# A transformer layer with a planned instruction order: GpSimd's queue in the plan, fewer gathers of softmax statistics, rows of the first norm moved to the gate products, earlier value sums, and the square root's table asked for ahead

## The chip, the cores and the metric

The kernel runs on one core of one Trainium2 chip. The metric is the device time of one execution in microseconds (us). The engines are TensorE (PE: matmuls and transposes, with PEld for its weight loads), VectorE (DVE), ScalarE (ACT), GpSimd (POOL) and SyncE (SP). SP does nothing here but issue DMA transfers, in a fixed order; POOL issues DMAs too, and hardly anything else. Every engine works through its own instructions strictly in order: where one waits, all behind it wait.

## The reference, cut to what matters

One layer over 1024 positions of width 1024 in fp32: a feed-forward part and norm 1, a mixer of attention and Fourier branch and norm 2, a second feed-forward part and norm 3.

```python
def swiglu(x, w_gate, w_up, w_down):
    return (jax.nn.silu(x @ w_gate) * (x @ w_up)) @ w_down          # inner width 2752

def hybrid_mixer(x, ...):
    h = x @ w_in + b_in                     # q, k, v (12 heads of 128), fourier channels, gates
    gates = jax.nn.sigmoid(...)
    for g, (window, dilation) in enumerate(((128, 1), (512, 4), (2048, 16))):
        o, l = dilated_window_attention(q_g, k_g, v_g, rel_bias_g, window, dilation)   # 4 heads
    w_mix = jax.nn.softmax(jnp.stack(lses, axis=0), axis=0)   # weights of the three groups
    attn = jnp.sum(w_mix[..., None] * jnp.stack(outs, axis=0), axis=0)
    four = jnp.real(jnp.fft.fft2(uf, axes=(1, 3), norm='ortho'))
    merged = g_attn * (attn @ w_proj_attn) + g_four * (four @ w_proj_fourier)
    return merged @ w_out

h = layer_norm(ALPHA * h + 0.5 * swiglu(h, ffn1...), ln1_g, ln1_b)
h = layer_norm(ALPHA * h + hybrid_mixer(h, ...), ln2_g, ln2_b)
h = layer_norm(ALPHA * h + 0.5 * swiglu(h, ffn2...), ln3_g, ln3_b)
```

## The kernel before, in words

**Products.** Each large product is cut into 2 x 2 blocks and done in seven block products, as in Strassen's scheme. They need sums of weight blocks and sums of products. An fp32 operand is split into a high and a low part (`ga` becomes `ga12h` on ACT and `ga12l` on DVE), and PE multiplies high by high, low by high and high by low. `Aa`, `Ab`, `Da`, `Db`, `Aq`, `Dq` are PSUM banks of such products; `t2a`, `t3a`, `sga` and the like are copies and sums that ACT and DVE make of them. `tpZ` and `pt` are transposes on PE. In the names, the first feed-forward part carries `a` at the end, the second `b`, the queries and keys `q`.

**Stages.** First feed-forward part (0 to about 580 us of the profile), with gate and up products in chunks, each chunk with weights `ga` and `ua` that SP loads; norm 1; values (`v`); queries, keys and attention together, head by head (about 820 to 1145); the gate products (about 1145 to 1280) with the Fourier branch's work after them; the output projection `wo` with norm 2 (about 1400 to 1470); the second feed-forward part and norm 3.

**Sums in DRAM.** Some sums of weight blocks are made by transfers: SP copies a block to a scratch tensor and POOL adds a second block by an accumulating DMA. `tdat` and `tdbt` are the sums for the down products, `vtt` those for the values (`t1`, `t3`, `t2`, `t4`, where `t2` starts from `t1` and `t4` from `t2`). A copy that starts from an earlier sum waits on SP's queue until that sum has landed.

**Attention.** Per head: scores (`sc`) on PE, bias and maximum on DVE (`p`, `stat`), exponentials on ACT (`p<-p,stat`), transposes of `p` on PE (`pt`), copies by ACT (`pT`), products with the values (`pv`). The maxima and sums go to DRAM (`stat`), and come back in another layout by gathers (`comb_t`); DVE and ACT make from them the weights of the three groups (`comb`), which are stored, broadcast over the partitions by POOL's DMA (`cb`) and multiplied into the stored outputs on DVE (`pw<-pw,cb`).

**Norm rows.** Norm 1 leaves rows without gain and bias in DRAM. Eight steps of `norm_rows` load such a tile `n`, multiply by the gain and add the bias on DVE, and spill it as `y_spill` from POOL's queue for the residual sum before norm 2.

**What sets the order.** The class `Flow` runs at build time. The code registers jobs of PE, tasks of DVE (`V`) and ACT (`S`), loads (`Q`) and floating PE work (`F`), with a cost in us, what they depend on, and a need: the job they must be ready for. `Flow` walks through the jobs with a clock for each of DVE and ACT and one for the transfers, picks the next task that is ready, and calls its function, which emits its instructions. The costs only order the instructions; nothing of them is executed. Buffers are counted in the same walk: 46 pages of 128 x 1024, 11 halves, 8 PSUM banks. A DMA that POOL issues was an ACT task of cost 0:

```python
n = S(0.0, lambda: nc.gpsimd.dma_start(dst, st["y"]), [n])
```

Of the kernel before, what the change touches and what calls it, by code (L numbers as in the profile page):

```python
# [72 lines left out]
class Flow:  # L73
# [3 lines left out]
    def __init__(self):  # L77
        self.jobs, self.tasks, self.loads, self.floats = [], [], [], []
        self.open = {"V": [], "S": []}
        self.clock = {"V": 0.0, "S": 0.0}  # L80
        self.pe = self.dma = self.now = 0.0
        self.pool = {"b": [0.0] * 8, "p": [0.0] * NPG, "h": [0.0] * NS2}
# [15 lines left out]
    def S(self, *a, **kw):  # L98
        return self.task("S", *a, **kw)

# [65 lines left out]
    def issue(self):  # L166
        for n in list(self.loads):
# [10 lines left out]
            t = max(self.pe, n.time(), self.take(n))  # L178
            n.fn()
            self.dma = max(self.dma, t) + n.cost / self.RATE  # L180
            self.finish(n, self.dma + self.LAND)

    def advance(self, until):
        while True:
            e = min(("V", "S"), key=lambda k: self.clock[k])
# [17 lines left out]
            if best is None or best[1] > c + 0.05:  # L203
                o = self.clock["S" if e == "V" else "V"]
# [5 lines left out]
            self.take(n)  # L210
            n.fn()
            self.clock[e] = r + n.cost
# [26 lines left out]
    def run(self):  # L239
# [9 lines left out]
        for i in range(4000):  # L249
            if not (self.floats or self.loads or self.open["V"] or self.open["S"]):  # L250
                break
# [33 lines left out]
def kernel(  # L285
# [10 lines left out]
    V, S, Q, F, job = fl.V, fl.S, fl.Q, fl.F, fl.job  # L296
# [14 lines left out]
    nc.vector.memset(eps, LN_EPS)  # L311

# [294 lines left out]
    def ffn(tag, X, w_gu, w_tail, w_dn, load_rest, norm, rest_deps=None, sums_at=None, by_tile=False):  # L607
# [7 lines left out]
        def spill(name, j, t):  # L615
            nc.gpsimd.dma_start(hs[name, j], t)  # L616
# [152 lines left out]
        for si, (to, x0, x1) in enumerate(sums):  # L769
            for i in range(3):  # L770
# [3 lines left out]
                def add(to=to, x1=x1, i=i):  # L774
                    nc.gpsimd.dma_start(td[to, i], dn(x1, i), accum_op=OP.add, max_dma_last_dim=4096)
# [28 lines left out]
        def step(p, j, set_, first):  # L804
# [10 lines left out]
            return run  # L815

# [140 lines left out]

    def norm_head(acc, sums, deps, name, which):
# [17 lines left out]
    def norm_tile(acc, sums, deps, name, which):  # L976
# [10 lines left out]
        return S(1.08, scaled, [n], gives=1), lambda: st["y"]  # L987

    def norm_rows(which, m, src, deps, dst, need):
# [15 lines left out]
        n = S(0.0, lambda: nc.gpsimd.dma_start(dst, st["y"]), [n])  # L1005
# [55 lines left out]
    def norm1(m, acc, sums, deps):  # L1061
        n, y = norm_tile(acc, sums, deps, f"y1_{m}", 1)
        unit[1, m] = S(0.0, lambda: nc.gpsimd.dma_start(n_spill[m], y()), [n])
# [18 lines left out]
    def mixer_consts():  # L1082
        st = {}

        def loads():
            st["raw"] = half("b_raw")[:56, :P]
            nc.gpsimd.dma_start(st["raw"], b_in.rearrange("(j p) -> j p", p=P))
            st["rb"], st["oh"] = kb.small([NUM_BUCKETS, NH], "rb"), half("oh")[:NUM_BUCKETS, :3 * NOFF]
            nc.gpsimd.dma_start(st["rb"], rel_bias)
            nc.gpsimd.dma_start(st["oh"], c_onehot.rearrange("b g o -> b (g o)"))  # L1090
            nc.gpsimd.dma_start(chan, c_chan)
            nc.gpsimd.dma_start(ln_cols, c_ln)
# [9 lines left out]
        def lines(g):  # L1102
# [3 lines left out]
            nc.gpsimd.dma_start(lines_d[:, g, :], line)  # L1106

        def shears(h):
            src = lines_d[h, h // SLOTS, :]
            nc.gpsimd.dma_start(shear_d[h], bass.AP(tensor=src.tensor, offset=src.offset, ap=[[0, P], [1, LINE]]))  # L1110
        q = S(0.0, loads, [J[("a", 6), 1]], slack=20.0, halves=2)
# [5 lines left out]
        return [S(0.0, lambda h=h: shears(h), [(n, 6.0 + 3.0 * h)]) for h in range(NH)]  # L1117

    def reversed_rows():
        idx = kb.small([P, 2], "rev_idx", mybir.dt.int32)  # L1120
        st, n = {}, S(0.0, lambda: nc.gpsimd.dma_start(idx, c_rev), [J[("a", 8), 1]], slack=20.0)
        for t in range(2):
            def gather(t=t):
                st[t] = page(f"rev{t}")
                nc.gpsimd.indirect_dma_start(out=st[t], out_offset=None, in_=w_pf,
                                             in_offset=bass.IndirectOffsetOnAxis(ap=idx[:, t:t + 1], axis=0))

            def store(t=t):
                nc.gpsimd.dma_start(w_rev[t * P:(t + 1) * P, :], st[t])
            n = S(0.0, gather, [(n, 16.0)], slack=20.0, pages=1)  # L1130
            n = S(0.0, store, [(n, 16.0)], slack=20.0)
# [40 lines left out]
    for i, (to, x0, x1) in enumerate((("t1", "b11", "b12"), ("t3", "b12", "b22"), ("t2", "t1", "b22"),  # L1172
# [4 lines left out]
        def add(to=to, x1=x1):  # L1177
            nc.gpsimd.dma_start(vt[to], vblk[x1], accum_op=OP.add, max_dma_last_dim=4096)
        n = Q(J[("a", 7 + i), 1], 1.0, copy, [vtn[x0]] if x0 in vtn else [], lead=0.0)
        vtn[to] = Q(J[("a", 8 + i), 5], 1.0, add, [n], lead=0.0)  # L1180

    def value_row(key, g, need):
        def run():
            vb[key] = half(f"vb{key}")
            nc.gpsimd.dma_start(vb[key], bcast_rows(b_in[COL_V + g * 512:COL_V + (g + 1) * 512], 512))
# [9 lines left out]
    def store_values(t, m, g):  # L1195
        nc.gpsimd.dma_start(v_d[m * P:(m + 1) * P, g * 512:(g + 1) * 512], t)
# [176 lines left out]
    def channel_parts(gi, get, deps, gives):  # L1373
# [18 lines left out]
        def parts():  # L1392
# [13 lines left out]
            nc.gpsimd.dma_start(uf_d[gi], uf)  # L1406
# [31 lines left out]
    def load_bias(g, h):  # L1438
# [3 lines left out]
        def shear(dst, base, rows, w):  # L1442
            nc.gpsimd.dma_start(dst, bass.AP(tensor=src.tensor, offset=src.offset + base,
# [42 lines left out]
    def attention(idx, g, h, qk, qk_nodes):  # L1486
# [17 lines left out]
        def one(si, step):  # L1504
# [105 lines left out]
        pv_n[g, h] = S(0.0, lambda: nc.gpsimd.dma_start(pv_d[g, h], env["pv"]), done_values)  # L1610
# [15 lines left out]
    for c in range(8):  # L1626
        gs = {}
        nodes = pair_out(PC["s", c], [COL_G + c * P, COL_G + D + c * P], gs, plain_view, AF.Sigmoid)
        for w in range(2):
            gate_n[w, c] = S(0.0, lambda c=c, w=w, gs=gs: nc.gpsimd.dma_start(gate_d[w, c], gs[w]), nodes[w])  # L1630
            fl.later(gate_n[w, c], 5.0, gives=1)

# [20 lines left out]
    def keep_parts(name, load, deps, fold_=None):  # L1653
# [15 lines left out]
        def store():  # L1669
            for i in range(2):  # L1670
                nc.gpsimd.dma_start(dst[i], st["p"][i].bitcast(F32))
        n = split(name + "e", lambda: st["r"], lambda p: st.__setitem__("p", p), [q], early, 52.0)
        n = S(0.0, store, [n])
# [34 lines left out]
    def combine(h):  # L1708
# [3 lines left out]
        def store():  # L1712
            nc.gpsimd.dma_start(stat_d[h], stats[h].rearrange("p c a -> p (c a)"))

        def gathers():
# [3 lines left out]
            def gather(dst, col, p0, ap):  # L1719
                nc.gpsimd.dma_start(dst, bass.AP(tensor=sd.tensor, offset=sd.offset + 48 * p0 + 2 * col, ap=ap))  # L1720

            for i in range(8):
# [459 lines left out]
```

## Time and profile before

| | us |
|---|---|
| three runs | 2089.58, 2090.97, 2095.2 (median 2090.97) |
| the profiled execution | 2091.19 |
| its span, first to last instruction | 2089.4 |
| PE busy (share of the span) | 2065.3 (99%) |
| DVE busy | 1276.3 (61%) |
| ACT busy | 906.5 (43%) |
| POOL busy | 246.8 (12%) |
| granted clock of PE, mean | 0.997 |

The time of an execution is that of its span and a little around it (1.8 us here). Busy time overlaps between engines. An engine's share is a mean over stages. "Granted clock" is the share of PE's full clock that it was allowed.

### The profile page before, as it was taken

The page shows a single profiled execution, that of the slowest core. Times are in us where ns is not written, and L with a number is a line of the kernel's source. Part 1 is how long each engine was busy: PE and PEld are TensorE (multiplying, and loading weights), DVE is VectorE, ACT ScalarE, POOL GpSimd, SP SyncE. Part 2 cuts the span into 40 slices and gives each one's busy share as a digit, 9 for nine tenths or more (in the row PEclk, how much of TensorE's full clock was granted, in tenths as well). Part 3 has the DMA queues.
Part 4 walks back from the last instruction along what each step waited for, and adds up shares of the span by engine and source line. Part 5 has one row for each costly group of instructions (what it writes and reads, how often), then busy time and mean ns, then how long its engine had stood idle before and what let it go on. Part 6 is the DMA issues. An engine that isn't in the chain of part 4 may idle for free.

```text
span 2089.4 us, 25573 instructions
## 1 busy us (share of the span) xinstructions
PE 2065.3 (99%) x9523; PEld 1715.0 (82%) x9523; DVE 1276.3 (61%) x1757; ACT 906.5 (43%) x1437; POOL 246.8 (12%) x432
## 2 busy tenths in 40 slices
PE   9999899999999999999999999999999999999998
PEld 7888788888888888888888888888888888888887
DVE  7765455676554657456655554763877665565565
ACT  6433233455475324445455443218733333355342
POOL 0123111111000010033131110000011111010000
PEclk9999999999999999999999999999999999999999
DMA  5469976599743336678784549433154533357743
GB/s 202 150 221 281 303 205 176 160 355 408 264 168 107 110 121 182 183 218 239 237 229 141 162 161 354 169 103 124 59 183 152 184 131 117 127 185 286 262 157 105
DMA packets 152124, 401.29 MB, mean 192 GB/s; under 512 B 19234, under 2 KB 41522, under 8 KB 151552
## 3 DMA queue, kind: packets, MB, share of 16 engines
q1 hardware_dynamic: 111648, 266.38, 36.3%
q0 software_dynamic: 40352, 133.29, 21.3%
q8 instruction: 74, 1.21, 0.2%
q14 instruction: 50, 0.41, 0.1%
HBM read 303.41 MB, written 153.84 MB: 219 GB/s over the span
## 4 chain that ended last, share of the span: by engine, by line
PE 89%; issue 3%; DMA 3%; ACT 3%; DVE 1%; POOL 1%; SPq 0%; DVEq 0%; POOLq 0%
PE Ab L447 13%; PE Aa L447 13%; PE Aq L447 6%; PE Db L447 5%; PE Da L447 5%; PE As L447 5%; PE Zb L812 3%; PE Xb L812 3%; PE Za L812 3%; PE Xa L812 3%; PE Dq L447 2%; PE pj L1964 2%; PE v L1214 2%; PE Ds L447 2%; PE vB L1153 2%
## 5 line engine op out<-in xcount | busy, mean ns | idle before, releaser
L1542 ACT ACTIVATE p<-p,stat 128x192 f32<-128x192 f32 (+2 forms) x96 | 42.2, 441 | 24.0 <-DVE stat L1537 23.4
L616 POOL DMA_DIRECT2D hsaa<-t2a x21 | 11.9, 569 | 316.0 <-DVE t2a L681 302.8
L616 POOL DMA_DIRECT2D hsba<-t2b x21 | 11.4, 543 | 281.1 <-DVE t2b L681 274.6
L1529 DVE SCALAR_TENSOR_TENSOR p<-sc,bias 128x512 f32<-128x512 f32 (+1 forms) x40 | 24.8, 620 | 31.9 <-PE sc L1515 30.5
L1574 PEld LDWEIGHTS pv<-pT,v 128*128 128x128 f32 (+1 forms) x320 | 37.1, 189 | 6.4 <-ACT pT L1563 1.4
L677 DVE TENSOR_TENSOR t2b<-Db,t2b 128x512 f32<-128x512 f32 x21 | 14.5, 691 | 44.5 <-PE Db L447 44.5
L1574 PE MATMUL pv<-pT,v 128*128 128x128 f32 (+1 forms) x320 | 40.7, 289 | 0.6 <-ACT pT L1563 0.4
L585 ACT ACTIVATE t2a<-Aa 128x512 f32<-128x512 f32 x21 | 12.6, 600 | 62.8 <-PE Aa L447 62.7
L677 DVE TENSOR_TENSOR t2a<-Da,t2a 128x512 f32<-128x512 f32 x21 | 14.5, 691 | 39.9 <-PE Da L447 39.9
L585 ACT ACTIVATE t2b<-Ab 128x512 f32<-128x512 f32 x21 | 12.6, 598 | 60.6 <-PE Ab L447 60.6
L1334 DVE SCALAR_TENSOR_TENSOR oq<-Dq,b_cols,t2q 128x512 f32<-128x512 f32 x12 | 11.8, 983 | 42.2 <-PE Dq L447 42.2
L1515 PE MATMUL sc<-oq,oq 128*128 128x192 f32 (+2 forms) x192 | 34.1, 322 | 0.0
L1515 PEld LDWEIGHTS sc<-oq,oq 128*128 128x128 f32 x192 | 29.8, 190 | 1.9
L1720 POOL DMA_DIRECT2D comb_t<-stat x48 | 29.3, 616 | 14.1 <-DMA tdbt<-in_ffn_down_dram 5.3
L447 PE MATMUL Db<-Zs40h,usb 128*128 128x512 f32 x84 | 29.4, 390 | 1.1 <-DVE t3b L669 1.1
L669 DVE TENSOR_TENSOR t3a<-Da,t3a 128x512 f32<-128x512 f32 x21 | 14.5, 690 | 25.5 <-PE Da L447 19.5
L447 PE MATMUL Da<-Xs40h,usa 128*128 128x512 f32 x84 | 29.4, 390 | 0.0
L447 PE MATMUL Db<-Zs41h,usb 128*128 128x512 f32 x84 | 29.3, 389 | 0.0
L447 PE MATMUL Da<-Xs41h,usa 128*128 128x512 f32 x84 | 29.3, 389 | 0.0
L585 ACT ACTIVATE t2q<-Aq 128x512 f32<-128x512 f32 x11 | 6.6, 597 | 49.8 <-PE Aq L447 49.8
L669 DVE TENSOR_TENSOR t3b<-Db,t3b 128x512 f32<-128x512 f32 x21 | 14.5, 690 | 21.9 <-PE Db L447 16.0
L1558 PE MATMUL pt<-ident,p 128*128 128x128 f32 x140 | 22.0, 280 | 4.7 <-ACT p L1542 4.2
(7339 smaller groups left out, 7216.8 us busy)
## 6 DMA issues: line engine op xcount, KB each, us to landing
qa<-hsas SPq DMA_DIRECT2D x44, 256.0 KB, 5.6
qa<-tdat SPq DMA_DIRECT2D x44, 256.0 KB, 5.1
qb<-hsbs SPq DMA_DIRECT2D x44, 256.0 KB, 4.0
ga<-in_ffn_gu_dram SPq DMA_DIRECT2D x21, 512.0 KB, 6.0
ua<-in_ffn_gu_dram SPq DMA_DIRECT2D x21, 512.0 KB, 7.2
gb<-in_ffn_gu_dram SPq DMA_DIRECT2D x21, 512.0 KB, 3.5
ub<-in_ffn_gu_dram SPq DMA_DIRECT2D x21, 512.0 KB, 4.5
qa<-hsaa SPq DMA_DIRECT2D x33, 256.0 KB, 4.0
```

The lines of the kernel that those rows point to most:

```text
L447: nc.tensor.matmul(out, pick(w, a)[:, k * P:(k + 1) * P], self.cols(xn, b, k), start=first and k == 0 and ti == 0, stop=last and k == 3 an ...
L585: nc.scalar.activation(H[c, t], B[c, "B"], AF.Copy)
L669: nc.vector.tensor_sub(H[c, "t3"], B[c, "D"], H[c, "t3"])
L677: nc.vector.tensor_sub(H[c, "t2"], B.pop((c, "D")), H[c, "t2"])
L812: nc.tensor.matmul(B[tag, set_, m], pick(q, a)[:, m * P:(m + 1) * P], pick(q, b)[:, R], start=first and j == 0 and ti == 0, stop=j == PAIR ...
L1153: nc.tensor.matmul(B["v", bk, m], X2.cols(xn, a, k)[:, m * P:(m + 1) * P], pick(w, b), start=new and k == 0 and ti == 0, stop=k == 3 and t ...
L1214: nc.tensor.matmul(ps, X2.cols(f"a{hf + 1}{k // 4 + 1}", a, k % 4)[:, mm * P:(mm + 1) * P], pick(wv, b), start=(k == 0 and ti == 0), stop= ...
L1515: nc.tensor.matmul(sv[:, i, :], qk[0][:, qt * P:(qt + 1) * P], qk[1][:, k0:k0 + w], start=True, stop=True, skip_group_check=True)
L1542: nc.scalar.activation(p3()[:, i, :], p3()[:, i, :], AF.Exp, bias=stats[h][:, k, 0:1], scale=1.0, accum_out=stats[h][:, k, 1:2])
L1574: nc.tensor.matmul(out_of(tiles.index(qt)), env["v"][kc, rows], pt[r0:r0 + rows, sl * P:(sl + 1) * P], start=qt not in seen, stop=last, sk ...
L1720: nc.gpsimd.dma_start(dst, bass.AP(tensor=sd.tensor, offset=sd.offset + 48 * p0 + 2 * col, ap=ap))
L1964: nc.tensor.matmul(bk[hf], pick(wv, a)[:, k, cc * P:(cc + 1) * P], pick(attn[k], b)[:, hf * 512:(hf + 1) * 512], start=(k == 0 and ti == 0 ...
```

## The change

The diff has five parts.

1. `Flow` gets a third queue, `G`, for POOL. Tasks that issue POOL's DMAs become `G` tasks, and `pool_dma` adds 0.57 us to that queue's clock for each transfer (0.95 for an accumulating one, 1.06 for an indirect one). This alone emits no instruction; it changes the order that the walk finds.
2. The copies and adds of `vtt` are needed six chunks earlier, by the walk's numbers.
3. Eight of the twelve gathers of a head's statistics become one. For this the two tiles 0 and 7 of the first group write their maxima and sums in exchanged columns, so that one access pattern covers all.
4. The eight `norm_rows` of norm 1, their constants and their spills are needed by the gate products, no longer by the query and key products.
5. `root_table` issues a square root of one column on ACT, whose only effect is that ACT's table for the square root is loaded: once behind a job of the first feed-forward part, and once at the first Fourier projection (`FJ[0]`). The planned cost of a norm's second `y` pass goes from 1.08 to 1.4.

```diff
+    def G(self, *a, **kw):
+        return self.task("G", 0.0, *a, **kw)
+
+    def queued(self, us):
+
+        self.clock["G"] = max(self.clock["G"], self.at) + us
...
+    def pool_dma(*a, **kw):
+        fl.queued(0.95 if "accum_op" in kw else 0.57)
+        nc.gpsimd.dma_start(*a, **kw)
...
+        if tag == "a":
+            root_table(J[tl, 1])
...
+    def root_table(after_):
+
+        t = kb.small([P, 1], "root", bufs=2)
+        S(1.5, lambda: nc.scalar.activation(t, eps, AF.Sqrt), [after_])
...
-        return S(1.08, scaled, [n], gives=1), lambda: st["y"]
+        return S(1.4, scaled, [n], gives=1), lambda: st["y"]
...
-        n = S(0.0, lambda: nc.gpsimd.dma_start(dst, st["y"]), [n])
+        n = G(lambda: pool_dma(dst, st["y"]), [n])
...
-            n = S(0.0, gather, [(n, 16.0)], slack=20.0, pages=1)
-            n = S(0.0, store, [(n, 16.0)], slack=20.0)
+            n = G(gather, [(n, 20.0)], slack=20.0, pages=1)
+            n = G(store, [(n, 30.0)], slack=20.0)
...
-        n = Q(J[("a", 7 + i), 1], 1.0, copy, [vtn[x0]] if x0 in vtn else [], lead=0.0)
-        vtn[to] = Q(J[("a", 8 + i), 5], 1.0, add, [n], lead=0.0)
+        n = Q(J[("a", 1 + i), 4], 1.0, copy, [vtn[x0]] if x0 in vtn else [], lead=0.0)
+        vtn[to] = Q(J[("a", 2 + i), 3], 1.0, add, [n], lead=0.0)
...
+            turned_round = g == 0 and tiles == [0, 7]
...
-                cols = slice(s0, s0 + stepc * (n - 1) + 1, stepc)
+                cols = slice(7, None, -7) if turned_round else slice(s0, s0 + stepc * (n - 1) + 1, stepc)
...
-                    k = s0 + i * stepc
+                    k = 7 - 7 * i if turned_round else s0 + i * stepc
...
-    for m in range(8):
-        spilled[1, m] = norm_rows(1, m, n_spill[m], [(unit[1, m], 5.0)], y_spill[m], J[PC["q", m + 3], 1])
-    ln_consts(1, ln1_g, ln1_b, J[PC["q", 3], 1])
...
+    for m in range(8):
+        spilled[1, m] = norm_rows(1, m, n_spill[m], [(unit[1, m], 5.0)], y_spill[m], J[PC["s", m], 1])
+    ln_consts(1, ln1_g, ln1_b, J[PC["s", 0], 1])
...
+    root_table(FJ[0])
...
-            for i in range(8):
-                gather(t[8 * i:8 * i + 8, 0], {0: 7, 7: 0}.get(i, i), 0, [[16 * 48, 8], [48, 16], [1, 2]])
+            gather(t[:, 0], 0, 0, [[2, 8], [16 * 48, 8], [48, 16], [1, 2]])
...
-            nc.gpsimd.dma_start(comb_d[h].rearrange("g (a f) -> a g f", f=16), e)
-        n = S(0.0, store, exp_n[h], slack=20.0)
-        n = S(0.0, gathers, [(n, 5.0)], slack=20.0)
+            pool_dma(comb_d[h].rearrange("g (a f) -> a g f", f=16), e)
+        n = G(store, exp_n[h], slack=20.0)
+        n = G(gathers, [(n, 5.0)], slack=20.0)
```

PE, DVE and SP issue the same instructions as before in another order. ACT has two more activations (`root<-eps`) and two more table loads, and POOL has 28 fewer DMAs.

**SP in the first feed-forward part.** In the rows, `ga` and `ua` are the weights of a chunk; the digit behind the name is the chunk. Before:

```order
L521 DMA ga_1841<-in_ffn_gu_dram 128x1024
L521 DMA ua_1843<-in_ffn_gu_dram 128x1024
L772 DMA tdat_190<-in_ffn_down_dram 16x16384
L1175 DMA vtt_216<-vtt_214 16x16384
L521 DMA ga_1985<-in_ffn_gu_dram 128x1024
```

After:

```order
L1199 DMA vtt1_214<-in_in_values_dram 16x16384
L536 DMA ga4_912<-in_ffn1_gu_dram 128x1024
L536 DMA ua4_932<-in_ffn1_gu_dram 128x1024
L1199 DMA vtt3_216<-in_in_values_dram 16x16384
L536 DMA ga5_1059<-in_ffn1_gu_dram 128x1024
L536 DMA ua5_1061<-in_ffn1_gu_dram 128x1024
L1199 DMA vtt2_215<-vtt1_214 16x16384
L536 DMA ga6_1138<-in_ffn1_gu_dram 128x1024
L536 DMA ua6_1140<-in_ffn1_gu_dram 128x1024
L1199 DMA vtt4_217<-vtt2_215 16x16384
L536 DMA ga7_1277<-in_ffn1_gu_dram 128x1024
```

The last copy stood ahead of the weights of chunk 12 and stands now ahead of those of chunk 7; the first stood ahead of chunk 9 and stands ahead of chunk 4.

**DVE in the attention stage.** `pw<-pw,cb` weighs a head, `p<-sc,bias` and `stat<-p` make scores and maxima ready for the exponentials, `gq13l` is a split of weights. Before:

```order
L1537 TENSOR_REDUCE stat<-p_8668 128x2
L565 TENSOR_TENSOR usq_8662<-uq_8423,usq_8662 128x512
L1766 TENSOR_TENSOR pw_8605<-pw_8605,cb_8603 128x512
L1769 TENSOR_TENSOR pw_8503<-pw_8503,pw_8605 128x512
L1529 SCALAR_TENSOR_TENSOR p_8711<-sc_8687,bias_8409 128x512
L335 TENSOR_TENSOR gq13l<-gq_8620,gq13h 128x1024
L1529 SCALAR_TENSOR_TENSOR p_8719<-sc_8690,bias_8409 128x384
```

After:

```order
L350 TENSOR_TENSOR gq13l<-gq_8476,gq13h 128x1024
L1553 SCALAR_TENSOR_TENSOR p_8606<-sc_8584,bias_8364 128x512
L1563 TENSOR_REDUCE stat<-p_8606 128x2
L1553 SCALAR_TENSOR_TENSOR p_8612<-sc_8587,bias_8364 128x512
L1563 TENSOR_REDUCE stat<-p_8612 128x2
L580 TENSOR_TENSOR usq_8604<-uq_8341,usq_8604 128x512
L552 TENSOR_TENSOR t12q_8651<-gq_8476,uq_8543 128x512
L1553 SCALAR_TENSOR_TENSOR p_8655<-sc_8628,bias_8364 128x512
L1553 SCALAR_TENSOR_TENSOR p_8657<-sc_8631,bias_8364 128x384
```

The weighing that stood ahead of the second pair of scores stands some ten instructions later, and the split ahead of the first pair.

**ACT around norm 2.** `y` is a norm's pass over a tile, `lnrs` its root, `Za` a copy of the transposed tile. Before:

```order
L331 ACTIVATE wo7h<-wo_11186 128x1024
L970 ACTIVATE y_0_11372,lw<-ya_10737,lw 128x1024
L972 ACT_TABLE_LOAD
L972 ACTIVATE lnrs_11374<-lw,eps 128x1
L985 ACTIVATE y_0_11372<-ya_10737,lw,lnrs_11374 128x1024
```

After, first at the Fourier projection and then at norm 2:

```order
L2032 ACTIVATE pfq_10631<-pfs_10608 128x512
L979 ACT_TABLE_LOAD
L979 ACTIVATE root<-eps 128x1
L346 ACTIVATE mg0h<-gl_10117 128x1024
```

```order
L346 ACTIVATE wo7h<-wo_11162 128x1024
L993 ACTIVATE y_0_11348,lw<-ya_10713,lw 128x1024
L995 ACTIVATE lnrs_11350<-lw,eps 128x1
L1008 ACTIVATE y_0_11348<-ya_10713,lw,lnrs_11350 128x1024
```

The load left its place between the first `y` and its root. In the first feed-forward part a load and a root come in behind the tail's products, and a second load brings Silu's table back ahead of the next `sga`; the load at norm 1 stays.

More of the change, by code (lines that the diff above doesn't have):

```diff
@@ L178, in issue @@
             t = max(self.pe, n.time(), self.take(n))
+            self.at, g = t, self.clock["G"]
             n.fn()
+            if self.clock["G"] > g:
+                t = max(t, self.clock["G"])
             self.dma = max(self.dma, t) + n.cost / self.RATE
@@ L184, in advance @@
         while True:
-            e = min(("V", "S"), key=lambda k: self.clock[k])
+            e = min(self.clock, key=lambda k: self.clock[k])
             c = self.clock[e]
@@ L203, in advance @@
             if best is None or best[1] > c + 0.05:
-                o = self.clock["S" if e == "V" else "V"]
+                o = min(self.clock[k] for k in self.clock if k != e)
                 stop = min(until, best[1]) if best is not None else until
@@ L210, in advance @@
             self.take(n)
+            self.clock[e] = self.at = r + n.cost
             n.fn()
-            self.clock[e] = r + n.cost
             self.finish(n, self.clock[e])
@@ L249, in run @@
         for i in range(4000):
-            if not (self.floats or self.loads or self.open["V"] or self.open["S"]):
+            if not (self.floats or self.loads or any(self.open.values())):
                 break
@@ L774, in add @@
                 def add(to=to, x1=x1, i=i):
[L775 removed]
+                    pool_dma(td[to, i], dn(x1, i), accum_op=OP.add, max_dma_last_dim=4096)
                 k = 3 * si + i
@@ L1124, in gather @@
                 st[t] = page(f"rev{t}")
+                fl.queued(1.06)
                 nc.gpsimd.indirect_dma_start(out=st[t], out_offset=None, in_=w_pf,
@@ L1930, in mid_raw @@
         for p0 in (0, 32, 64):
-            nc.gpsimd.dma_start(raw[p0:p0 + 4, :], rows)
+            pool_dma(raw[p0:p0 + 4, :], rows)
     def mid_weights():
```

63 lines of the change are left out of this document (32 added, 31 removed).

## The prediction

> **What bounds the kernel now.** I read the page's engine shares and its chain first, to learn which engine sets the end, then the waits of that engine, then a table of stretches of the span, and last the timelines of the engines around the largest waits.
>
> ```profile
> PE 2065.3 (99%) x9523; PEld 1715.0 (82%) x9523; DVE 1276.3 (61%) x1757; ACT 906.5 (43%) x1437; POOL 246.8 (12%) x432
> PE 89%; issue 3%; DMA 3%; ACT 3%; DVE 1%; POOL 1%; SPq 0%; DVEq 0%; POOLq 0%
> ```
>
> PE works for 2065.3 of 2089.4 us and is 89% of the chain that ended last. The diff changes no matmul, so nothing can be won but PE's idle time, some 24 us, and the time in which its clock was lowered behind such idleness. The waits of PE (line waited at, what it waited for; us in total, times, longest) tell where most of it lies:
>
> ```profile
> PE Aa L447 <- ACT t3a L585: 6.2, 1, 6.2
> PE pt L1558 <- ACT p L1542: 4.2, 5, 1.4
> PE tpZ L392 <- ACT y L985: 1.7, 5, 0.6
> ```
>
> One wait in the first feed-forward part, five in the attention stage, five at the second norm. The stretches around the first two (columns: us, busy us of PE, PEld, DVE, ACT, POOL with instruction counts, granted PE clock, DMA share, GB/s):
>
> ```profile
> 55.00:130.00 75.00, 75.00 (x333) 62.10 (x332) 55.57 (x76) 27.13 (x39) 14.13 (x26) 1.00 0.43 152
> 200.00:231.50 31.50, 31.50 (x140) 26.10 (x139) 14.12 (x19) 8.17 (x12) 8.03 (x12) 1.00 1.05 290
> 236.00:243.30 7.30, 5.22 (x13) 4.12 (x14) 3.94 (x5) 2.60 (x3) 0.00 (x0) 0.53 1.04 342
> 820.00:900.00 80.00, 78.85 (x414) 66.34 (x413) 43.89 (x57) 43.66 (x102) 8.57 (x14) 1.00 0.73 208
> 900.00:950.00 50.00, 48.53 (x251) 40.83 (x250) 28.20 (x45) 24.12 (x63) 14.04 (x24) 1.00 0.73 198
> 1060.00:1100.00 40.00, 38.23 (x185) 31.44 (x184) 20.46 (x33) 17.41 (x39) 12.26 (x21) 0.96 0.83 225
> 1086.00:1090.00 4.00, 4.00 (x13) 3.11 (x12) 3.57 (x9) 2.31 (x5) 0.56 (x1) 0.57 0.22 56
> 1100.00:1150.00 50.00, 49.56 (x263) 41.66 (x262) 26.42 (x38) 29.11 (x69) 8.58 (x15) 1.00 0.46 139
> 1150.00:1280.00 130.00, 130.00 (x578) 107.70 (x577) 67.74 (x91) 59.69 (x81) 18.29 (x32) 1.00 0.56 194
> ```
>
> Elsewhere PE is covered, so a step moved into a covered stretch costs nothing until it uses up the cover. Now the change by its places.
>
> **1. The value sums (`vtt`) leave the loads' way.** The 6.2 us wait, on PE, ACT, SP's and POOL's queues and as a piece of the chain:
>
> ```profile
> 231.29 0.39 PE L447 MATMUL Da<-Xs11l,t12a11h 128*128 128x512 f32 x1
> 231.52 0.39 PE L447 MATMUL Da<-Xs11h,t12a11l 128*128 128x512 f32 x1
> 238.08 0.79 PE L447 MATMUL Aa<-Xa220h,t34a11h 128*128 128x512 f32 x1 [6.17 <-ACT t3a L585]
> 236.48 1.06 ACT L331 ACTIVATE ga12h<-ga 128x1024 fp32r<-128x1024 f32 x1 [9.38 <-DMA ga<-in_ffn_gu_dram]
> 228.74 0.47 SPq L1175 DMA_DIRECT2D vtt<-vtt  x1
> 229.32 0.51 SPq L521 DMA_DIRECT2D ga<-in_ffn_gu_dram  x1
> 214.64 14.08 DMA vtt<-in_in_values_dram
> ```
>
> Read upwards from the last row: an accumulating transfer started at 214.64 and landed at 228.72; SP stood before its copy `vtt<-vtt` until then; the weight load `ga` queued behind that copy left at 229.32, ACT split it at 236.48, `t3a` stands behind that on ACT, and PE stands behind `t3a`. PE's starts lie 6.56 us apart where 0.23 is usual (the two rows before), so 6.33 us of waiting. In 236.0 to 243.3 the clock was 0.53: 0.47 x 7.30 = 3.4 us, of which half of the 2.08 us before PE started is no loss, leaving 2.4. Together 8.7 us.
>
> The change issues all four copies (SP) and four adds (POOL) some five weight chunks earlier, in a stretch where the transfer engines are busy 0.43 of the time instead of 1.05. Nothing is left between SP and `ga` of chunk 12, so I count the whole 8.7. What is late next? The last copy now stands before `ga` of chunk 7. Its chain, from rows:
>
> ```profile
> 76.19 1.14 POOL L616 DMA_DIRECT2D hsas<-sba  x2
> 101.36 1.08 POOL L616 DMA_DIRECT2D hsas<-sba  x2
> 108.16 0.33 SPq L521 DMA_DIRECT2D ga<-in_ffn_gu_dram  x1
> 122.49 1.05 ACT L331 ACTIVATE ga7h<-ga 128x1024 fp32r<-128x1024 f32 x1
> tdat<-in_ffn_down_dram POOLq DMA_DIRECT2D x8, 1024.0 KB, 9.8
> vtt<-in_in_values_dram POOLq DMA_DIRECT2D x4, 1024.0 KB, 20.6
> DMA to landing us min/median/max: 5.7/9.5/10.5
> ga<-in_ffn_gu_dram SPq DMA_DIRECT2D x21, 512.0 KB, 6.0
> ```
>
> (The last four: median us to landing of adds of the same 1 MB in the first feed-forward part, of the value adds, of the value copies on SP's line 1175, and of `ga`.) The first add goes out behind the spills that end at 77.3, the chained copy after it, the second add behind the spills that end at 102.4. Taking 9.8 for an add, since this stretch is half empty: 77.3 + 9.8 + 9.5 = 96.6, before 102.4; 102.4 + 9.8 = 112.2, then copy and `ga` leave, and `ga` lands 6.0 later at about 118.8, 3.7 us before ACT wants it at 122.49. Behind ACT lie another 9.38 - 6.17 = 3.2 us before PE feels it. So nothing is lost at 9.8; at 20.6 both times: 77.3 + 20.6 + 9.5 = 107.4, + 20.6 + 0.6 + 6.0 = 134.6, 12.1 late, 8.9 on PE. I take 0 and keep 8.9 as a rival. Chunk 6's `ga` too stands behind a chained copy, which can go at 77.3 + 9.8 = 87.1, two chunks' work before ACT's row of chunk 7: 0, and part of the same rival.
>
> **2. The attention stage.** Three kinds of delay feed the five `pt` waits:
>
> ```profile
> 858.77 0.63 ACT L561 ACTIVATE usq<-uq 128x512 fp32r<-128x512 f32 x1 [3.21 <-PE Aq L447]
> 912.02 1.06 ACT L331 ACTIVATE gq7h<-gq 128x1024 fp32r<-128x1024 f32 x1 [3.12 <-PE Aq L447]
> 913.62 0.93 PE L1558 MATMUL pt<-ident,p 128*128 128x128 f32 x4 [1.41 <-ACT p L1542]
> 1065.58 0.60 POOL L1720 DMA_DIRECT2D comb_t<-stat  x1 [5.34 <-DMA tdbt<-in_ffn_down_dram]
> 1077.96 0.69 DVE L1766 TENSOR_TENSOR pw<-pw,cb 128x512 f32<-128x512 f32 x1 [5.44 <-DMA cb<-comb]
> L1720 POOL DMA_DIRECT2D comb_t<-stat x48 | 29.3, 616 | 14.1 <-DMA tdbt<-in_ffn_down_dram 5.3
> L1001 DVE TENSOR_TENSOR n<-n,ln1b x8: 1218/1224/1226, 865.7 to 1054.0; 128x1024 f32<-128x1024 f32 x8
> ```
>
> At 858 and 912 ACT stood 3.2 and 3.1 us at a split that waited for a matmul of PE, because its page came free only then; the exponentials that PE's `pt` needs were queued behind it. At 1077.96 DVE stood 5.44 us before weighing a head (`pw`), since `cb`, a broadcast on POOL's queue, came late: POOL was held in the gathers of statistics (12 per head, 616 ns each, and waits between them). Scores and maxima were queued behind, and PE waited twice.
>
> The change takes the eight rows' gain and bias work (8 x 2 x 1.22 = 19.6 us of DVE), its pages, its loads on SP and its spills on POOL out of this stage; it replaces 8 of 12 gathers per head by one; and it counts POOL's time, which puts `pw` later in DVE's order. One gather over 64 rows is bounded by 0.56 to 0.71 us (the shortest and longest of line 1720 now) and 8 x 0.6 = 4.8; I take 0.8, nearest the longest, as it only has more pieces than that one: 4 us less of POOL per head. POOL is busy 12%, so this counts only through `cb`.
>
> Worth: idle PE in the four stretches 1.15 + 1.47 + 1.77 + 0.44 = 4.8; the clock of 0.57 in 1086 to 1090, 0.43 x 4.0 = 1.7; and a refill of about 0.2 us at each of the five places, 1.0 (an estimate; no row shows it apart, and without it the sum is 6.5). Sum 7.5, with 0.5 left in stretches not shown: 8.0 at most. Transposes that wait for exponentials stay, as the order is tight there, and `cb` still takes microseconds to land: I leave 1.0 and take 7.0; the ends are 0 and 8.0.
>
> On the clock the Trainium skill (TensorE: Matmul & The Clock Gate, Part 1) says that PE drops to half rate after at least one idle window of some 3.4 us. The 6.2 us wait agrees. The drop at 1086 does not: no PE wait in the stage is above 1.4 us. By the page's rule the drop would have another cause and stay, and the sum would be 1.7 us smaller, 2076.7; by the row, several short waits close together suffice.
>
> **3. Norm rows under the gates.** They stand now in 1150 to 1280, DVE 67.7 + 19.6 = 87.3 of 130 us, 67%, as in the covered stretch 55 to 130 (74%). PE never waits there today. Cost 0; ends 0 and, as a rival, 33.
>
> **4. The square root's table ahead of norm 2.**
>
> ```profile
> 1414.87 1.28 ACT L972 ACT_TABLE_LOAD   x1
> 1416.17 0.29 ACT L972 ACTIVATE lnrs<-lw,eps 128x1 f32<-128x1 f32 x1
> 1418.18 1.09 PE L392 MATMUL tpZ<-ident,y 128*128 128x128 f32 x8 [0.59 <-ACT y L985]
> ```
>
> The 1.28 us load stood between `y` and its root, in the path to PE's transpose. It goes to the Fourier projection, where ACT has little to do. The 0.59 us wait goes; with the longer planned `y`, one more of about 0.5 should. I take 1.0 of the 1.7 us in the waits' row; ends 0 and 1.7.
>
> The same function in the first feed-forward part does not do what it says: a Silu stands behind it, so the table is loaded back, and norm 1 still loads its own. Two more loads and a root, 2 x 1.28 + 0.29 = 2.9 us of ACT, where ACT is busy 18.54 of 30 us:
>
> ```profile
> 400.00:430.00 30.00, 30.00 (x134) 24.85 (x133) 23.86 (x28) 18.54 (x23) 3.24 (x6) 1.00 0.68 241
> ```
>
> Its idle time, 11.5 us, hides them; without it PE would lose up to 2.9. The Trainium skill (ScalarE: Activation LUTs, What ACT_TABLE_LOAD costs) adds a drain of 1.38 us to each switch, 2.66 in all; by it ACT would spend 5.6 us here, and the uncovered loss would be 2.7 larger. The trace does not show that drain behind a load: the root starts at 1416.17, 0.02 us after the load's end. I cost the step at 0.
>
> **5. The rest.** Reversed rows wait longer between gather and store, read much later: 0. New orders on PE, DVE and ACT bring new short waits; 0.5, ends 0 and 4 (one stall like that of 1077).
>
> **Sum.** -8.7 - 7.0 - 1.0 + 0.5 = -16.2 us against the profiled execution of 2091.19 us (span 2089.4), which is 0.2 above the median of the runs, 2090.97. That gives 2075.0.
>
> **Rivals.**
> - *The value sums stall chunk 7 instead.* For it: every value add took 14 us or more, and their median is 20.6. Against: they ran at a share of 1.05. It bites when the mean add exceeds about 9.8 + (3.7 + 3.2) / 2 = 13.2 us. At 20.6: + 8.9 and, as at 238, 2.4 of clock: 2086; at 16: 2081. Chance 0.13.
> - *The attention waits stay.* `pw` still stands at DVE's head when `cb` is late, or ACT's exponentials still come late in the new order. For it: `cb` can't land before its gathers, and the chain of gather, shares and broadcast is as long as before but for 4 us. With 6 of the 7.0 kept: 2081. Chance 0.11.
> - *Slower: the rows' DVE work makes PE wait in every gate chunk.* 8 chunks lie in that stretch, and 2.44 us in front of the piece PE needs, with 1.7 of clock as at 1086, are 4.1 each, 33 us: 2108. It cancels the gain at 2.0 us per chunk. Against it: DVE is at 67%. Chance 0.05.
> - *The page's clock rule*: 2076.7, 0.1 within the main case.
>
> **How the numbers follow.** Main case 0.70, 2075, its own range 2071 to 2080 (all of 8.7 + 8.0 + 1.7, or new waits of 4 and no gain at norm 2). The three rivals have 0.29, others 0.01. The range reaches down to 2069.5, since short waits in other stretches may close too, and up to 2086.5, the first rival's end; the slower one is left out. A measurement of this kernel tells about 0.3%, 6.3 us, from no change: faster means below 2084.7. Main case and some six tenths of the first two rivals' chances there give 0.85; full stalls and half-cancelled gains 0.10; slower 0.05.
>
> **What would show it.** Right: no `Aa <- t3a` wait of 6 us, and the clock at 1.00 around 240; SP's last `vtt` copy before 118 with `ga` of chunk 7 landed before 122; value adds landing in about 10 us; `pt <- p` waits of about 1 us in all; no DVE idle time before `pw` above 2 us; DVE at two thirds under the gates with PE unbroken; twelve table loads, none before the first `lnrs` of norm 2. Wrong: a new wait of `Aa` near 125; clock below 1.00 between 820 and 1280; or a wait of PE for DVE's pieces in each gate chunk.

## The result, and the profile after

The changed kernel takes 2071.92 us (median of four runs, 2071.32 to 2072.24) against 2092.22 us (four runs, 2089.58 to 2095.2) for the kernel before: ratio 0.9902, 95% interval 0.9885 to 0.9919. The profiled executions differ by 2091.19 - 2072.24 = 18.95 us where 16.2 was forecast, and 2071.92 lies inside the range, at the low end of the likeliest case.

The page's shares and chain, and all waits of PE above 0.4 us but the one at the start:

```profile
PE 2058.5 (99%) x9523; PEld 1713.6 (83%) x9523; DVE 1276.4 (62%) x1757; ACT 910.4 (44%) x1441; POOL 233.6 (11%) x404
PE 97%; ACT 1%; DMA 1%; DVE 0%; issue 0%; DVEq 0%; SPq 0%
```

```profile
PE Db L462 <- DVE t3b L684: 0.7, 1, 0.7
PE tpZ L407 <- ACT y L1008: 0.6, 3, 0.2
PE Aa L462 <- ACT Xa110h L361: 0.6, 1, 0.6
PE pv L1600 <- ACT pT L1589: 0.5, 1, 0.5
```

The waits of `Aa` for `t3a` (6.2 us) and of `pt` for `p` (4.2 us) are gone, and PE is 97% of the chain that ended last instead of 89%. The same stretches as before:

```profile
55.00:130.00 75.00, 75.00 (x333) 62.10 (x332) 55.48 (x76) 27.80 (x40) 17.85 (x30) 1.00 0.84 253
200.00:231.50 31.50, 31.50 (x140) 26.09 (x139) 17.58 (x23) 11.27 (x16) 7.34 (x11) 1.00 0.90 271
236.00:243.30 7.30, 7.30 (x34) 6.01 (x34) 3.99 (x6) 1.70 (x3) 0.81 (x2) 1.00 0.00 1
820.00:900.00 80.00, 80.00 (x423) 67.91 (x421) 38.99 (x53) 43.02 (x102) 11.27 (x17) 1.00 0.65 171
900.00:950.00 50.00, 50.00 (x270) 42.36 (x269) 26.79 (x44) 27.83 (x70) 7.22 (x12) 1.00 0.58 162
1060.00:1100.00 40.00, 40.00 (x219) 34.22 (x218) 24.27 (x42) 20.63 (x54) 6.72 (x11) 1.00 0.76 214
1100.00:1150.00 50.00, 49.47 (x245) 41.15 (x245) 32.58 (x47) 28.53 (x52) 11.42 (x19) 1.00 0.59 184
1102.00:1262.30 160.30, 159.77 (x724) 132.64 (x725) 99.37 (x125) 76.21 (x117) 27.61 (x48) 1.00 0.65 227
```

The transfer engines' share (the mean busy share of the 16 DMA engines) rose from 0.43 to 0.84 in 55 to 130, where the value sums stand now. PE is unbroken from 820 to 1100 with its full clock. The last row is the whole stage of the gate products after the change: DVE is busy 99.4 of 160.3 us.

The place on which the first rival hung, SP's copies and loads, POOL's first and third adds (those that the copies wait for), ACT's split of chunk 7, and the adds' median time to landing:

```profile
77.97 1.04 POOL L326 DMA_DIRECT2D vtt<-in_in_values_dram  x1
91.02 0.48 SPq L1199 DMA_DIRECT2D vtt<-vtt  x1
103.58 0.99 POOL L326 DMA_DIRECT2D vtt<-in_in_values_dram  x1
114.13 0.48 SPq L1199 DMA_DIRECT2D vtt<-vtt  x1
114.79 0.44 SPq L536 DMA_DIRECT2D ga<-in_ffn_gu_dram  x1
123.13 1.05 ACT L346 ACTIVATE ga7h<-ga 128x1024 fp32r<-128x1024 f32 x1
vtt<-in_in_values_dram POOLq DMA_DIRECT2D x4, 1024.0 KB, 11.8
```

The last copy left at 114.13 (112.2 worked out), `ga` at 114.79, and ACT split it at 123.13 without an idle row ahead of it. It was close: the median `ga` of 60 to 140 takes 7.9 us to land, so that this one came at about 122.7 (an estimate).

Because the order of the stages' first products hardly differs, the time of a stage can be read from the starts of first matmuls in the traces: `Aa` to `Xa` for the first feed-forward part, `sc` to `wo` for attention, gates and branches, `wo` to `Db` for norm 2. The profiled executions (us) and the medians of each kernel's runs:

| kernel | Aa to Xa | sc to wo | wo to Db | median |
|---|---|---|---|---|
| before | 422.27 | 529.91 | 135.84 | 2091 to 2093 |
| after | 413.56 | 520.86 | 134.40 | 2071.92 |
| after, sums late (e1) | 427.77 | 520.88 | 134.33 | 2086.51 |
| after, rows in attention (e2) | 413.29 | 526.71 | 134.34 | 2077.42 |
| after, eight gathers (e3) | 414.98 | 520.85 | 134.37 | 2072.49 |
| after, POOL uncounted (e5) | 413.43 | 520.29 | 134.37 | 2071.75 |
| after, no root (e4) | 413.23 | 520.70 | 135.13 | 2072.12 |
| after, two more passes (e6) | 413.69 | 520.87 | 134.33 | 2071.88 |
| after, four more passes (e7) | 414.26 | 533.40 | 134.35 | 2085.00 |
| before, sums early (b1) | 413.97 | 528.58 | 135.79 | 2080.97 |
| before, rows under the gates (b2) | 421.70 | 521.94 | 135.83 | 2084.57 |
| before, one gather (b3) | 423.37 | 524.56 | 135.84 | 2086.08 |
| before, POOL counted (b4) | 425.52 | 526.33 | 135.75 | 2090.41 |
| before, sums and rows (b6) | 413.92 | 521.39 | 135.83 | 2075.44 |

So the change took 8.71 us off the first stage, 9.05 off the second, 1.44 off the third. The first column holds the start of the kernel too, where kernels without the wait of `Aa` for `t3a` differ by up to 1.75 us (413.23 to 414.98), and those with a wait of 6 to 7 us nearly as much (before, b2, b3: 421.70 to 423.37). The time of the kernel before also varies more than that of the changed one: 2088.33 to 2096.42 us over all its runs.

### The profile page after: what moved, and what is told of

Its sections match the earlier page's. It is cut to its first block, busy times and chain, and to the rows that moved or that the text cites. A ratio compares the mean times of both kernels' runs of the same rounds, so it can differ in the third digit from the quotient of the medians.

```text
span 2070.3 us, 25541 instructions
## 1 busy us (share of the span) xinstructions
PE 2058.5 (99%) x9523; PEld 1713.6 (83%) x9523; DVE 1276.4 (62%) x1757; ACT 910.4 (44%) x1441; POOL 233.6 (11%) x404
## 4 chain that ended last, share of the span: by engine, by line
PE 97%; ACT 1%; DMA 1%; DVE 0%; issue 0%; DVEq 0%; SPq 0%
PE Ab L462 14%; PE Aa L462 13%; PE Aq L462 8%; PE Da L462 6%; PE Db L462 5%; PE As L462 5%; PE wo L2078 3%; PE Dq L462 3%; PE Zb L827 3%; PE Xb L827 3%; PE Za L827 3%; PE Xa L827 3%; PE pj L1991 2%; PE v L1238 2%; PE Ds L462 2%; PE pv L1600 2%
## 5 line engine op out<-in xcount | busy, mean ns | idle before, releaser
L1358 DVE SCALAR_TENSOR_TENSOR oq<-Dq,b_cols,t2q 128x512 f32<-128x512 f32 x12 | 11.8, 986 | 50.8 <-PE Dq L462 50.8
L1553 DVE SCALAR_TENSOR_TENSOR p<-sc,bias 128x512 f32<-128x512 f32 (+1 forms) x40 | 24.7, 620 | 25.0 <-PE sc L1539 20.6
L326 POOL DMA_DIRECT2D n_spill<-y x16 | 8.6, 538 | 264.5 <-ACT y L1008 264.5
L1358 DVE SCALAR_TENSOR_TENSOR oq<-Dq,b_cols,t3q 128x512 f32<-128x512 f32 x12 | 11.8, 987 | 30.1 <-PE Dq L462 30.1
L1563 DVE TENSOR_REDUCE stat<-p 128x2 f32<-128x384 f32 (+2 forms) x40 | 24.5, 620 | 1.2
```

The lines of the kernel that those rows point to most:

```text
L326: nc.gpsimd.dma_start(*a, **kw)
```

## The experiments

**The value sums, taken back and alone.** e1 undoes their move in the changed kernel, b1 makes it alone in the kernel before:

```diff
-        n = Q(J[("a", 1 + i), 4], 1.0, copy, ...)
-        vtn[to] = Q(J[("a", 2 + i), 3], 1.0, add, ...)
+        n = Q(J[("a", 7 + i), 1], 1.0, copy, ...)
+        vtn[to] = Q(J[("a", 8 + i), 5], 1.0, add, ...)
```

> The changed kernel with the value sums needed at the old chunks (copies ahead of chunks 9 to 12), all else as changed. Theory (the 8.7 us of the first feed-forward part come from the place of these sums alone): the wait of PE behind SP's last copy returns with its slow clock, +8.7 us, 2080.6. Rival (counting POOL in the order, or the one gather, already keeps POOL's queue from holding the sums): under +2 us, 2072 to 2074, and no wait of Aa for t3a above 2 us.

> The kernel before with nothing but the needs of the value sums moved to the early chunks. Theory (the sums alone carry the first stage): -8.7 us against before, about 2083.5 on this chip's 2092, the attention waits as before. Rival (SP or POOL needs the counting too, so a wait at chunk 7 or 8 comes): 2086 to 2092.

e1: 2086.51 us (2085.09 to 2087.7), 14.6 more than the change. b1: 2080.97 (2077.67 to 2081.73), ratio to before 0.9936 (0.9919 to 0.9952). The wait of PE in e1, and the chain at that place (start, us, what):

```profile
PE Aa L462 <- ACT t3a L600: 11.6, 1, 11.6
```

```profile
195.55 22.98 DMA vtt<-in_in_values_dram
...
218.81 13.37 DMA vtt<-in_in_values_dram
...
232.20 0.47 SPq L1199
...
232.79 10.14 DMA ga<-in_ffn_gu_dram
```

The sums' place is the cause: put back, the wait returns at the same product, and moved alone, it goes (8.3 us of the first column). Its size is not a constant: in e1 two adds in a row took 23.0 and 13.4 us and `ga` 10.1, at a share of the transfer engines of 1.04 (200 to 232.5), and the stage is 14.2 us longer, not 8.7. The counting of POOL may have a part in that: b4, with counting and late sums, has a `t3a` wait of 9.3 us against 6.2 before, in one profile each. The rival, that counting or the one gather would keep SP free, fell. The attention waits of b1 are not those of before, as its theory had it: PE waits three times for `p`, 4.5 us in all, where before it was five times and 4.2.

**The attention stage, part by part.** In the changed kernel, e2 puts the norm rows back under the query and key products, e3 the eight gathers, and e5 lets POOL's transfers add nothing to its clock:

```diff
 e2
-        spilled[1, m] = norm_rows(1, m, ..., J[PC["s", m], 1])
-    ln_consts(1, ln1_g, ln1_b, J[PC["s", 0], 1])
+        spilled[1, m] = norm_rows(1, m, ..., J[PC["q", m + 3], 1])
+    ln_consts(1, ln1_g, ln1_b, J[PC["q", 3], 1])
 e3
-            gather(t[:, 0], 0, 0, [[2, 8], [16 * 48, 8], [48, 16], [1, 2]])
+            for i in range(8):
+                gather(t[8 * i:8 * i + 8, 0], i, 0, [[16 * 48, 8], [48, 16], [1, 2]])
 e5
-        self.clock["G"] = max(self.clock["G"], self.at) + us
+        pass
```

> The changed kernel with the eight norm rows needed by the query and key products again, one gather and POOL counted as changed. Theory (two halves of the attention gain: ACT's splits that wait for a page, 2.2 + 2.1 us at 858 and 912, come from the rows' pages; the rest from the weighing): +4.3 us, 2076, with an ACT split idle for 3 us ahead of exponentials, and no DVE wait for cb. Rival 1 (the rows are all of it): +9, 2081. Rival 2 (the gather and the counting are all of it): within 1 us of 2071.9.

> The changed kernel with eight gathers of 8 rows again in place of the one of 64 rows; rows under the gates and POOL counted as changed. Theory (the shorter gathers are what brings cb in time): DVE stands 4 us or so before a weighing in two of four heads, +4 to 6 us, 2076 to 2078. Rival (the order now places the weighing by POOL's counted time, so that a slower POOL only moves it later): within 1 us of 2071.9, and no DVE wait for cb above 1 us.

> The changed kernel with POOL's transfers adding nothing to its queue's clock at build time; one gather, rows under the gates, early sums and root tables as changed. Theory (the counting places the weighing late enough): the weighing stands early again and DVE waits for cb, some 5 us once or twice, PE loses 2 to 5 us, 2074 to 2077. Rival (with one gather and no spills of rows POOL is free enough): within 1 us of 2071.9.

e2: 2077.42 us (2076.07 to 2077.95), +5.5. e3: 2072.49 (2071.89 to 2074.23) and e5: 2071.75 (2071.07 to 2072.5), both the changed kernel's time. The wait of `pt` in e2, and ACT's splits ahead of it:

```profile
PE pt L1584 <- ACT p L1568: 3.7, 3, 1.4
```

```profile
850.27 0.63 ACT L576 ACTIVATE usq<-uq 128x512 fp32r<-128x512 f32 x1 [3.21 <-PE Aq L462]
903.58 1.06 ACT L346 ACTIVATE gq7h<-gq 128x1024 fp32r<-128x1024 f32 x1 [3.12 <-PE Aq L462]
1011.62 1.06 ACT L346 ACTIVATE gq11h<-gq 128x1024 fp32r<-128x1024 f32 x1 [2.63 <-PE Aq L462]
```

The two page waits of before return, with the same 3.21 and 3.12 us, and a third of their kind comes. DVE has no wait of `pw` for `cb` in e2's attention. So the pages of the rows are one cause, and the late `cb` is another, which the gather and the counting together remove with the rows still in place. Neither e3 nor e5 brings PE's waits back, and the theories of both fell. In e5 DVE waits longer for `cb` than in the changed kernel (second row), and PE has no `pt` wait for it:

```profile
DVE pw L1793 <- DMA cb<-comb: 5.4, 3, 2.8
DVE pw L1793 <- DMA cb<-comb: 3.1, 3, 1.4
```

That neither was missed could mean that neither counts, or that each does the other's work. So each part was put alone into the kernel before: b2 the rows, b3 the gather, b4 the counting (with the `G` tasks; rows, sums, gathers, roots and lead times as before).

> The kernel before with nothing but the eight norm rows needed by the gate products. Theory (the rows' move alone frees pages, DVE and POOL's queue): all 9.2 us of the attention stage, about 2083, no wait of pt above 0.3 us and no DVE wait for cb above 3 us. Rival (twelve gathers on POOL still bring cb late): 4 to 6 us, 2086 to 2088, with the waits at about 1000 and 1080 left.

> The kernel before with nothing but the eight gathers made one. Theory (any one of fewer gathers, counting, or rows moved brings cb in time, but only the rows free the pages): -5 us or so, 2087, the ACT page waits at 858 and 912 left, no DVE wait for cb above 2 us. Rival (the gather alone does nothing, as POOL waits for other landings): within 1 us of before, 2091 to 2092.

> The kernel before with nothing but POOL's queue counted in the build-time order. Theory (the weighing is placed later, page waits stay): -5 us or so in the attention stage, and the first stage within 6 us of before either way (the order of POOL there moves): 2083 to 2092. Rival (counting alone changes the order but removes no wait): attention stage within 1 us of before.

b2: 2084.57 us, ratio 0.9963 (0.9949 to 0.9977); b3: 2086.08, 0.9962 (0.9948 to 0.9976); b4: 2090.41, 0.9989 (0.9979 to 0.9999). Off the stage from `sc` to `wo`: rows alone 8.0 us, the gather alone 5.4, the counting alone 3.6; 17 together, where the whole change takes 9.05. The parts cover for each other. The waits of PE in the stage (first b2, then b3, then two of b4), and DVE's waits for `cb` over the whole span, in the kernel before and in b2, with the longest one of b2:

```profile
PE pt L1558 <- ACT p L1542: 0.5, 1, 0.5
```

```profile
PE pt L1560 <- ACT p L1544: 2.3, 2, 1.4
```

```profile
PE pv L1597 <- ACT pT L1586: 2.4, 1, 2.4
PE pt L1581 <- ACT p L1565: 0.9, 1, 0.9
```

```profile
DVE pw L1766 <- DMA cb<-comb: 9.5, 2, 5.4
DVE pw L1767 <- DMA cb<-comb: 10.6, 3, 6.1
1150.79 0.69 DVE L1767 TENSOR_TENSOR pw<-pw,cb 128x512 f32<-128x512 f32 x1 [6.07 <-DMA cb<-comb]
```

The rows alone end the page waits. They do not bring `cb` earlier: DVE waits 10.6 us for it in three places, more than the 9.5 of before. But the longest wait now falls among the gate products, where no wait of PE is above 0.2 us, and the one at 1064 (3.7 us) costs PE 0.5. So b2's theory fell where it had DVE wait no more than 3 us for `cb`, and its rival fell too, which had PE's waits near 1000 and 1080 stay with a late `cb`. The gather alone does bring `cb` in time (0.3 us of such waits in b3) and leaves the page waits. The counting alone leaves 4.3 us of waits for `cb`, removes PE's wait at 912 and those near 1080, and makes a new one of 2.4 us that ends at 1133.9; the kernel before has 0.4 there. In its new order ACT takes a sigmoid of the gate products (line 1347) between the last exponentials (line 1565), and changes its table twice for it:

```profile
1128.44 1.28 ACT L1347 ACT_TABLE_LOAD   x1 [0.45 <-PE As L462]
1130.44 1.28 ACT L1565 ACT_TABLE_LOAD   x1
```

A new order gives and takes.

**Two parts only.** b6 is the kernel before with the early sums and the rows under the gates.

> The kernel before with two parts only: the sums early and the rows under the gates. No counting of POOL, twelve gathers, no root, y at 1.08. Theory (these two carry all but norm 2, and the parts add): 8.7 + 8.4 us off, 1.4 short of the whole change, 2073 to 2075; pt and t3a waits gone, norm 2's 1.7 us of waits left. Rival (with the sums early POOL's order shifts and the twelve gathers bring cb late again, as counting or one gather would have kept it from doing): 2077 or more, with a wait of pt above 1 us.

b6: 2075.44 us (2074.14 to 2076.41), ratio 0.9928 (0.9911 to 0.9944). Its waits:

```profile
PE tpZ L392 <- ACT y L985: 1.6, 5, 0.6
PE Db L447 <- DVE t3b L669: 1.6, 1, 1.6
PE pt L1558 <- ACT p L1542: 0.4, 1, 0.4
```

Two of the five parts bring 8.4 and 8.5 us in their stages, against 8.7 and 9.05 for all. As in b2, `cb` still comes late (DVE waits 8.9 us for it), at places where PE loses only 0.4 us. What is missing is norm 2's 1.4, about 0.9 in the two stages, and about 1 in a wait of `Db` at 1851, a place that the change does not touch.

**The root.** e4 leaves out both `root_table` calls and keeps the planned 1.4 of `y`.

> The changed kernel without either of the two activations that ask for the square root's table; the longer planned y pass of 1.4 stays. Theory (the load between y and its root was 0.6 to 0.75 us of the 1.4 us gained at norm 2, the earlier place of a transpose the rest; the load in the first feed-forward part is worth nothing): +0.7 us, 2072.6, the first wait of tpZ back at 0.59, no change of PE's gaps near 400. Rival (the page's drain counts at 400 and costs PE today): faster by 1 us or more, below 2071. Either size is near what the runs can tell, so the waits of PE decide.

e4: 2072.12 us (2071.95 to 2073.62), not to be told from the change by its time. ACT's load is back between `y` and the root, and PE's waits for `y` grow from 0.6 us in three to 1.1 in four:

```profile
1396.81 1.28 ACT L992 ACT_TABLE_LOAD   x1
1398.10 0.29 ACT L992 ACTIVATE lnrs<-lw,eps 128x1 f32<-128x1 f32 x1
```

```profile
PE tpZ L407 <- ACT y L1005: 1.1, 4, 0.6
```

The stage from `wo` to `Db` takes 135.13 us: of the 1.44 us, 0.7 are the table. The other 0.7 go, by elimination, to the longer planned `y`, which puts one group of transposes earlier in PE's order: every kernel with `y` at 1.08 (before, b1 to b4, b6) takes 135.8 there. The two extra loads in the first part cost nothing that shows: 413.23 without them and 413.56 with them, within the spread of the start. (The drain in the expectation is that of the Trainium skill, ScalarE: Activation LUTs, What ACT_TABLE_LOAD costs. Here too the root starts 0.01 us after the load's end: no drain of 1.38 us stands between them.)

**How much cover the gates have.** e6 and e7 add two and four passes of DVE over each moved row, unknown to the plan; the passes change no value.

```diff
             nc.vector.tensor_add(st["y"], st["y"], LN[which][1])
+            for _ in range(2 if which == 1 else 0):          # e7: 4
+                nc.vector.tensor_tensor(out=st["y"], in0=st["y"], in1=st["y"], op=OP.max)
```

> The changed kernel with two more passes of DVE over each of the eight norm rows (a maximum of the row with itself, which changes no value), not planned as longer: 16 x 1.22 = 19.5 us more of DVE under the gates, 119 of 160 us. Theory (DVE has cover there): within 1 us of 2071.9. Rival (each pass stands in front of the piece that PE needs): + 8 x 2.4, 2091.

> The same with four more passes: 39 us more of DVE, 138 of 160 us (86%). Theory (cover by busy share lasts nearly to the end): under +4 us, below 2076, single waits of PE for DVE pieces. Rival (order counts, not share: 4.9 us in a row in front of a piece exceed the lead of every chunk): + 8 x (4.9 - 2.4) = 20 us and more with the clock, above 2090.

e6: 2071.88 us (2071.35 to 2072.61), no change. e7: 2085.0 (2083.91 to 2086.92), +13. The gates' stage of both, e6 first, and in e7 PE's waits and one place of them on DVE and ACT:

```profile
1102.00:1262.30 160.30, 159.77 (x725) 132.72 (x724) 117.06 (x141) 75.05 (x114) 27.52 (x48) 1.00 0.66 227
```

```profile
1102.00:1280.00 178.00, 169.03 (x748) 137.29 (x747) 139.82 (x160) 75.92 (x117) 28.07 (x49) 0.99 0.63 221
```

```profile
PE As L462 <- ACT t2s L600: 6.4, 5, 2.8
PE As L462 <- ACT t3s L600: 1.9, 1, 1.9
```

```profile
1151.66 5.01 DVE L1026 TENSOR_TENSOR n<-n 128x1024 f32<-128x1024 f32 x4
1158.63 0.72 ACT L1371 ACTIVATE os<-t2s,b_cols 128x512 f32<-128x512 f32 x1 [8.06 <-DVE t2s L1366]
```

With DVE at 73% of the stage nothing is lost; with four passes in a row (5.0 us) in front of `t2s`, ACT waits 8 us and PE's next product 2.8. The theory of cover by share, under 4 us, fell at the second dose: the stage had some 22 us of DVE time left in 160 and lost 12.5 all the same. At the place shown it is the stretch in one piece that outlasts the chunk's lead; that the same passes, spread out, would be hidden was not tried. The rival's 20 us were too many: PE waited six times, 8.3 us in all.

## Why the prediction was right

**The value sums: 8.7 forecast, 8.71 measured**, and e1 and b1 show that their place is the cause. That the two agree so closely is luck, as executions of like kernels differ by 1.7 us in this column. The step that took an add at 9.8 us and not at 20.6 held in its outcome: the two adds of the chain landed after 13.0 and 10.5 us (77.97 to 91.02 and 103.58 to 114.13), 11.8 in the mean, below the 13.2 from which the first rival would have bitten. Its reason did not hold: with the sums in it the stretch is not half empty. The share is 0.93 from 78 to 132, where the adds ran, and was 1.02 from 170 to 213 for the slow adds of before. The margin was thin: the forecast had `ga` of chunk 7 land 3.7 us before ACT wants it and named 122 as the latest, and it came at about 122.7, some 0.4 us before ACT's split.

**Attention: 7.0 forecast, 9.05 measured, above the 8.0 called the most.** The failed term is the refill. PE's idle time from 820 to 1150 fell by 4.8 us (5.3 to 0.5), the clock gave back 1.7, and 2.5 are left over, where 1.0 was guessed for five refills. Starts of PE in the kernel before show where such time lies. From 911.82 to 913.62 PE took 1.80 us for a step of 0.23, so it lost 1.57 where the wait column shows 1.41. And the transposes behind a wait come only as fast as ACT finishes their exponentials, which it starts 0.44 us apart there (859.30 to 860.62): six take 1.75 us behind the wait, and 0.87 where PE did not wait:

```profile
859.89 1.75 PE L1558 MATMUL pt<-ident,p 128*128 128x128 f32 x6 [0.93 <-ACT p L1542]
867.54 0.87 PE L1558 MATMUL pt<-ident,p 128*128 128x128 f32 x6
```

So much of the term is no refill of PE, but further waiting for ACT that the wait column does not show. The 1.0 kept for waits that stay was wrong too: the one that stayed was there before (0.4 us, now 0.5). As for the mechanisms, both were there, but the prediction shared the gain among three edits, and b2 to b4 show that one, the rows, would do nearly all. The three do not act alike on the late `cb`: the gather brings it in time (b3), and the other two change the order so that DVE's wait for it costs PE less, the rows without shortening that wait at all (b2). One gather over 64 rows also costs more than the 0.8 us taken: the longest of line 326 on `comb_t` takes 1.25 us, so that a head's five take 3.75.

```profile
L326 POOL DMA_DIRECT2D comb_t<-stat x20: 557/686/1250, 882.9 to 1122.2; - x20
```

**Norm rows under the gates: 0 forecast, 0 measured.** The slower rival did not come, and e6 shows that twice the rows would be hidden as well.

**Norm 2: 1.0 forecast, 1.44 measured**, half from the table and half from the planned `y`. The root in the first part cost and brought nothing, as forecast.

**New waits: 0.5 forecast, none above 0.3 us found.** The `Db` wait near 1850 is 0.7 us in the profile after and 1.1 before; over the experiments it varies from none (e3, e7) to 1.6 (b6), so I don't count it as a gain of the change. The three stages sum to 19.2 us.

## What to carry to other kernels

When an engine is busy 99%, find the wait, then the first instruction in the queues behind it that waits for something slow: here an accumulating transfer, three queues away from the matmul. Price a wait from start to start, with the slow work and the clock behind it, not by the wait column. Read waits over the whole span: an edit may move one past the edge of the stretch looked at, as the rows moved DVE's. And if several edits are aimed at one wait, put each alone into the old kernel as well as taking it out of the new one: taken out, two of three edits here were worth 0, and put in, 5.4 and 3.6 us.

## What the runs showed of the hardware

A wait of PE of 2 to 3 us can be followed by a lower clock. The single wait of 2.13 us in b1 was (994 to 998, first row), and so was one of 2.78 us in e7 (second row). A wait of 1.94 us in e7, which ended at 1268.99, was not (third row), nor were one of 1.62 us in b6 and those of 1.41 us in e2:

```profile
994.00:998.00 4.00, 4.00 (x13) 3.04 (x12) 3.92 (x8) 3.18 (x12) 0.00 (x0) 0.58 0.99 161
1161.50:1164.90 3.40, 3.40 (x10) 2.62 (x9) 2.24 (x5) 1.43 (x2) 0.00 (x0) 0.50 0.60 205
1268.00:1274.00 6.00, 5.00 (x22) 4.00 (x23) 4.18 (x4) 5.05 (x7) 0.56 (x1) 1.00 1.03 395
```

The length of the wait alone does not decide: in the kernel before, waits of 1.06 and 0.54 us close together, 1.60 in all, were followed by a clock of 0.57 (1086 to 1090). What else counts stays open. The Trainium skill (TensorE: Matmul & The Clock Gate, Part 1) names at least one idle window of some 3.4 us; the 2.13 us of b1 and the 2.78 us of e7 are less.

The landing time of an accumulating transfer of 1 MB is no property of the transfer: 11.8 us in the median for the four value adds of the changed kernel, 20.6 for those of before, 22.98 for one of e1. Nor does the share of the transfer engines tell it. The add issued at 170.77 in the kernel before landed after 20.6 us at a share of 1.01 (170.8 to 191.4), and the one issued at 121.18 in the changed kernel after 10.6 us, also at 1.01 (121.2 to 131.8). What does, no run here shows.
